# A stored table of priorities in place of a 60-pass search that orders the instructions of a two-layer encoder trunk

## The chip, the core and the metric

The kernel runs on one core of one Trainium2 chip. The metric is the device time of one execution, in microseconds. Lower is better.

## The reference

Two layers (DEPTH = 2) over 2048 frames of width 1024, all float32. Each layer normalises and modulates the frame, projects it once, mixes in two parallel groups of heads and adds the result to the residual:

```python
for l in range(DEPTH):
    mod = c_act @ w_ada[l] + b_ada[l]                       # shift, scale, gate
    h = rms_norm(x, norm_g[l]) * (1.0 + scale[:, None]) + shift[:, None]
    proj = h @ w_in[l]
    gq, gk, gv, glr, gz, dq, dk, dv, dz = split_columns(proj)
    gqkv = silu(causal_depthwise_conv(concat([gq, gk, gv]), conv_w[l]))
    o_gla  = gla_branch(...)    # 4 heads, chunks of 64: state = a*state + k_dec^T v ; o = q state ; rms_norm * silu(gz)
    o_diff = diff_branch(...)   # 4 heads, two softmax maps: p0 - lam*p1, block-causal ; rms_norm * silu(dz)
    x = x + gate[:, None] * (concat([o_gla, o_diff]) @ w_out[l])
```

## The kernel before

**Tiling.** The sequence is cut into NU = 4 units of 512 frames, so there are 8 unit passes (layer, unit). In each pass the normalised input stands as eight 128x512 tiles, each split into a high and a low part (`hhi`, `hlo`), and so is each weight tile (`w` holds both). A product in near-float32 precision is three matmuls: hi by hi, hi by lo, lo by hi. They add up in PSUM banks called `acc` (4 of them). Four more banks with the tag "tp" are shared by score tiles (`sc`), transposes (`tp`, matmuls against `ident`) and attention outputs (`po`).

**Streams.** Generators write the work down: the projections and the output projection (`acc<-...`); the gated linear attention (gate matmuls with `wglr`, cumulated gates with `trir`, transposes of `uT`, state products `sc<-vN,E` and `po<-Sn,qT`); the softmax attention of one head after another (scores `sc<-Kj,qh`, evicted by VectorE to `s` with a running minimum `mx`, exponential on ScalarE, transposes `tp<-ident,s`, their copy on ScalarE, then `po<-Vj,s` and `po<-Vt,s`; the result is scaled into `z` by a power `wq` that GpSimd makes, and transposed, `tp<-ident,z`, into `oh` and `ol`); the preparation of the next unit (`xt` is squared on ScalarE for the norm, `xp` times the norm gives `hhi`, `hlo`); and the modulation (`wr` loads multiplied into `am` on VectorE). In unit 0 of layer 0 the first norm is made in a special start: squares summed into `sqs`, a matmul with `ones`, `xms`, a power on GpSimd, `t` (a diagonal), a broadcast matmul, `rsb`, and the first modulation from `wm`.

**What sets the order.** Nothing of this is issued when it is written down. `Program.record` stores each operation with its dependencies, its buffers and a cost from a formula; there are 19,414 of them. `order(turn_of)` then runs a list scheduler over a model of the five queues: at each step the engine that is free first takes, among its operations that are ready, the one with the smallest number in `turn_of`. A tile is given a buffer when its turn in its pool has come, so pools bound how far work can run ahead. The order that comes out is issued as it is; each engine then works through its own list in that order, and waits where an operand is late. Loads and stores all stand in one list on SyncE's queue.

```python
            while pend[e] and pend[e][0][0] <= t:
                heapq.heappush(avail[e], heapq.heappop(pend[e])[1:])
```

In the kernel before, `turn_of` starts as the order of writing and is changed in 60 passes (`best_order`): where the model shows TensorE waiting, the chain behind the wait is moved up; a pass whose modelled span isn't longer is kept. All engine instructions of the computation carry the line of the one call in `issue` (L375 before, L351 in the changed kernel), so groups are told apart by tile names.

Of the kernel before, what the change touches and what calls it, by code (L numbers as in the profile page):

```python
# [4 lines left out]

# [11 lines left out]
AF = mybir.ActivationFunctionType  # L17
ALU = mybir.AluOpType
AX = mybir.AxisListType
# [3 lines left out]
P = 128  # L23
D = 1024
KT = D // P
UT = 512
TT = UT // P
# [23 lines left out]
class View:  # L51
# [57 lines left out]
    def real(self):  # L109
        ap = self.buf.tile  # L110
        for name, args, kw in self.path:
            ap = getattr(ap, name)(*args, **kw)
        return ap
# [10 lines left out]
class Program:  # L124
# [90 lines left out]
        func = op[2][2] if op[1] == "activation" else None  # L215
        return {AF.Exp: 0, AF.Tanh: 0, AF.Ln: 1}.get(func)

    def best_order(self, rounds=60):


        ops, rnd = self.ops, random.Random(0)
        turn = [float(i) for i in range(len(ops))]
        made = self.order(turn)
        best = self.span
        for _ in range(rounds):
            res, begin, end, ready, held = made
            lines = {e: [i for i in res if ops[i][0] == e] for e in "TAV"}
            place = {i: k for q in lines.values() for k, i in enumerate(q)}
            waits = [(begin[i] - end[j], i) for j, i in zip(lines["T"], lines["T"][1:]) if begin[i] - end[j] > 150]
            turn2 = list(turn)  # L230
            for wait, i in waits:
                if rnd.random() >= wait / 1500 * rnd.random():
                    continue
                first = begin[i] - 15000
                for _ in range(12):
                    e = ops[i][0]
                    i = max(ops[i][4] | {held.get(i, i)} - {i}, key=lambda j: end[j] + self.LAT[ops[j][0]][e], default=None)
                    if i is None or end[i] < first:
                        break
                    if (ops[i][0] in "AV" or ops[i][0] == "T" and i not in self.group) and begin[i] - ready[i] > 80:  # L240
                        q, k = lines[ops[i][0]], place[i] - 1
                        while k >= 0 and begin[q[k]] >= ready[i]:
                            turn2[i] = min(turn2[i], turn[q[k]] - 0.5)
                            k -= 1
            made2 = self.order(turn2)
            if self.span <= best:
                best, made, turn = self.span, made2, turn2
        self.span = best
        return made[0]

    def order(self, turn_of):
        ops, N = self.ops, len(self.ops)
# [114 lines left out]

    def issue(self):
        real = lambda v: v.real() if isinstance(v, View) else v
        for i in self.best_order():  # L370
            e, method, args, kw, _, _, bufs = self.ops[i]
            for b in bufs:
                if b.tile is None:
                    b.make()
            getattr(self.engines[e], method)(*[real(a) for a in args], **{k: real(v) for k, v in kw.items()})  # L375
# [988 lines left out]
        lam=np.stack([lam_q1, lam_k1, lam_q2, lam_k2], axis=1).reshape(1, -1))  # L1364


# [19 lines left out]
```

## Time and profile before

| what | value |
|---|---|
| median of 3 runs | 2448.12 us (2446.68 to 2451.21) |
| profiled execution | 2444.97 us, its span 2443.3 us |
| mean granted TensorE clock | 0.994 |
| TensorE busy | 2375.5 us (97%), 12903 matmuls |
| VectorE, ScalarE, GpSimd busy | 1828.8, 1240.2, 124.3 us |
| DMA | 573.77 MB, mean 235 GB/s |

An instruction's row gives engine, tile names (out<-in), shape and count. An fp32 product with a 128-column operand (`po`, the 64-row state products) appears as two matmuls each. The idle time of TensorE is what the span leaves beside its busy time; a matmul's row lasts longer than the distance to the next one's start, so short waits do not show as idle.

### The profile page before, as it was taken

How to read it: one execution, taken by the hardware profiler on the slowest of the kernel's cores; microseconds unless marked ns; L12 is line 12 of the kernel's file. 1: busy time of each engine (PE TensorE's matmuls, PEld its weight loads, DVE VectorE, ACT ScalarE, POOL GpSimd, SP SyncE). 2: the span in 40 equal slices, each digit the busy share in tenths (PEclk: the TensorE clock that was granted, in tenths of full speed). 3: DMA queues.
4: the chain of work that ended last, by engine and by line, in shares of the span. 5: the costliest groups of instructions: out<-in, count | busy, mean ns of one | idle time of the engine just before them, and what ended most of it. 6: DMA issues, size and time to landing. Idle time of an engine off the chain costs nothing.

```text
span 2443.3 us, 38591 instructions
## 1 busy us (share of the span) xinstructions
PE 2375.5 (97%) x12903; PEld 1941.1 (79%) x12903; DVE 1828.8 (75%) x5166; ACT 1240.2 (51%) x2726; POOL 124.3 (5%) x400
## 2 busy tenths in 40 slices
PE   6899899999999999999999999999999999999998
PEld 5687687887888878887788877888788887888787
DVE  8878776897568976589875887468864888738883
ACT  4776643566345553355664566255532555425442
POOL 0010000000000000000000010000000000000000
PEclk9899999999999999999999999999999999999999
DMA  7657897777766869487567877675686776866663
GB/s 298 234 208 253 283 341 249 238 260 250 250 228 207 253 192 300 162 243 210 189 219 272 287 249 261 228 242 191 221 273 215 233 226 220 248 227 203 195 206 126
DMA packets 369526, 573.77 MB, mean 235 GB/s; under 512 B 191824, under 2 KB 251696, under 8 KB 366256
## 3 DMA queue, kind: packets, MB, share of 16 engines
q1 hardware_dynamic: 369328, 571.32, 70.7%
q8 instruction: 102, 1.67, 0.3%
q14 instruction: 96, 0.79, 0.1%
HBM read 416.03 MB, written 161.50 MB: 236 GB/s over the span
## 4 chain that ended last, share of the span: by engine, by line
PE 75%; DVE 13%; DMA 5%; ACT 4%; issue 2%; POOL 0%; SPq 0%; POOLq 0%; DVEq 0%; ACTq 0%
PE acc L375 50%; PE sc L375 11%; PE po L375 9%; DVE s L375 6%; PE tp L375 4%; DMA wr<-in_w_ada_dram 2%; DVE t L375 1%; ACT s L375 1%; DVE w L375 1%; DMA xt<-in_x_dram 1%; ACT qh L375 1%; DVE am L375 0%; ACT t L375 0%; DVE r L375 0%; DMA xp<-xd 0%
## 5 line engine op out<-in xcount | busy, mean ns | idle before, releaser
L375 PE MATMUL acc<-w,hhi 128*128 128x512 f32 x2560 | 831.5, 401 | 5.9 <-ACT hhi L375 2.3
L375 PEld LDWEIGHTS acc<-w,hhi 128*128 128x128 f32 x2560 | 467.9, 189 | 98.2 <-DVE t L375 3.9
L375 PE MATMUL acc<-w,hlo 128*128 128x512 f32 x1280 | 507.3, 397 | 0.0
L375 ACT ACTIVATE s<-s,mx 128x512 f32<-128x512 f32 (+15 forms) x256 | 308.2, 1204 | 302.2 <-DVE s L375 152.7
L375 PE MATMUL acc<-oh,w 128*128 128x512 f32 x1024 | 357.7, 400 | 2.3 <-ACT oh L375 0.8
L375 DVE TENSOR_SCALAR_CACHE_REDUCE s<-sc,mx 64x64 f32<-64x64 f32 (+5 forms) x640 | 307.4, 483 | 48.1 <-PE sc L375 27.6
L375 PE MATMUL acc<-hhi,w 128*128 128x512 f32 x960 | 318.9, 398 | 0.0
L375 PEld LDWEIGHTS acc<-w,hlo 128*128 128x128 f32 x1280 | 241.9, 189 | 49.3 <-issue 1.1
L375 PEld LDWEIGHTS acc<-oh,w 128*128 128x128 f32 x1024 | 192.5, 189 | 44.4 <-DVE rt L375 3.2
L375 PEld LDWEIGHTS acc<-hhi,w 128*128 128x128 f32 x960 | 179.5, 188 | 36.3 <-DVE z L375 0.6
L375 PE MATMUL acc<-ol,w 128*128 128x512 f32 x512 | 201.9, 394 | 0.0
L375 PEld LDWEIGHTS po<-Vj,s 128*128 128x128 f32 x1536 | 193.4, 196 | 8.6 <-DMA s<-ad 1.7
L375 DVE SCALAR_TENSOR_TENSOR s<-s,r 128x512 f32<-128x512 f32 (+2 forms) x320 | 198.3, 666 | 2.3
L375 PE MATMUL po<-Vj,s 128*128 128x128 f32 x1536 | 198.5, 281 | 1.0 <-ACT s L375 0.7
L375 PE MATMUL acc<-hlo,w 128*128 128x512 f32 x480 | 189.0, 394 | 0.0
L375 DVE TENSOR_SCALAR_CACHE_REDUCE s<-sc 128x512 f32<-128x512 f32 (+4 forms) x256 | 157.9, 621 | 38.3 <-PE sc L375 29.0
L375 PE MATMUL sc<-Kj,qh 128*128 128x512 f32 x384 | 161.2, 420 | 6.0 <-DVE s L375 5.9
L375 PE MATMUL sc<-Kj,ql 128*128 128x512 f32 x384 | 152.2, 396 | 0.0
L375 ACT CAST w<-raw 128x512 fp32r<-128x512 f32 x160 | 97.8, 622 | 104.7 <-PE acc L375 84.1
L375 DVE TENSOR_TENSOR w<-raw,w 128x512 fp32r<-128x512 f32 x160 | 108.8, 686 | 45.9 <-ACT w L375 45.1
L375 DVE SCALAR_TENSOR_TENSOR t<-ub,vec,t 128x512 f32<-128x512 f32 x192 | 138.1, 746 | 6.0 <-ACT t L375 5.5
L375 POOL MEMSET s<- 64x64 f32 x256 | 36.9, 144 | 2020.0 <-PE po L375 1405.6
(185 smaller groups left out, 3590.2 us busy)
## 6 DMA issues: line engine op xcount, KB each, us to landing
w<-wd SPq DMA_DIRECT2D x416, 512.0 KB, 4.4
wd<-w SPq DMA_DIRECT2D x144, 512.0 KB, 4.1
raw<-in_w_all_dram SPq DMA_DIRECT2D x80, 512.0 KB, 4.8
Kj<-kd SPq DMA_DIRECT2D x48, 512.0 KB, 6.0
ad<-s SPq DMA_DIRECT2D x24, 768.0 KB, 5.6
s<-ad SPq DMA_DIRECT2D x24, 768.0 KB, 6.9
wr<-in_w_ada_dram SPq DMA_DIRECT2D x128, 128.0 KB, 4.3
ad<-s SPq DMA_DIRECT2D x32, 512.0 KB, 3.6
```

Source lines behind the costliest of these rows:

```text
L375: getattr(self.engines[e], method)(*[real(a) for a in args], **{k: real(v) for k, v in kw.items()})
```

## The change

`best_order` is gone. `found_order` unpacks a stored table of 19,414 small numbers, one for each recorded operation, sums them up and adds them to the order of writing; the result is `turn_of` for one call of `order`. The scheduler, its costs, the pools, the recorded operations, their number and their operands are unchanged; only the place of each in its engine's list differs.

```diff
-    def best_order(self, rounds=60):
-        ops, rnd = self.ops, random.Random(0)
-        turn = [float(i) for i in range(len(ops))]
-        made = self.order(turn)
-        best = self.span
-        for _ in range(rounds):
...
-            made2 = self.order(turn2)
-            if self.span <= best:
-                best, made, turn = self.span, made2, turn2
-        self.span = best
-        return made[0]
+    def found_order(self):
+        step = np.frombuffer(lzma.decompress(base64.b85decode(ORDER)), dtype="<i2")
+        turn = np.arange(len(self.ops), dtype=float)
+        if len(step) == len(turn):
+            turn += np.cumsum(step.astype(int))
+        return self.order(turn.tolist())[0]
...
-        for i in self.best_order():
+        for i in self.found_order():
...
+ORDER = (
+    '{Wp48S^xk9=GL@E0stWa8~^|S5YJf5;FqgLq+I|2U>bnck+!@@V3AjytBp45^Tr3;$E~Z9ORR0R@5I(P6(V1^7&ZjV2!e;h2L-hkd023f?~QmHvy'
...
```

On TensorE 5,222 of the 11,215 recorded operations keep their order among themselves; half of all stand at least 20 places away from where they stood. On VectorE it is 2,211 of 4,254 (half moved by 5 places or more), on ScalarE 1,210 of 2,313 (4), on SyncE 738 of 1,236 (3), on GpSimd 360 of 396. Both lists load ScalarE's tables 17 times. Three places, on which the prediction rests:

**The start, on VectorE**, from the last sums of squares (`sqs`) to the first `xp` and `hlo`. `wm` is the modulation, `w<-raw,w` the low part of a weight tile. Before:

```order
L375 TENSOR_TENSOR sqs<-t_195,sqs 128x512
L375 SCALAR_TENSOR_TENSOR wm,sv<-wm,cb 128x1024 x2
L375 TENSOR_SCALAR xms<-sc 128x4
L375 TENSOR_TENSOR B_217<-sv,vec 128x1
L375 SCALAR_TENSOR_TENSOR sv<-sv,vec 128x1
L375 TENSOR_TENSOR w<-raw,w 128x512
L375 TENSOR_TENSOR A_226<-sv,vec 128x1
L375 TENSOR_TENSOR w<-raw,w 128x512
L375 TENSOR_SCALAR t_231<-ident,rs_115 128x128 x4
L375 TENSOR_TENSOR w<-raw,w 128x512 x2
L375 SCALAR_TENSOR_TENSOR wm,sv<-wm,cb 128x1024
L375 SCALAR_TENSOR_TENSOR xp<-xp,A_226,rsb 128x512
```

Now:

```order
L351 TENSOR_TENSOR sqs<-t_205,sqs 128x512
L351 SCALAR_TENSOR_TENSOR wm,sv<-wm,cb 128x1024 x2
L351 TENSOR_TENSOR w<-raw,w 128x512 x2
L351 TENSOR_SCALAR xms<-sc 128x4
L351 SCALAR_TENSOR_TENSOR sv<-sv,vec 128x1
L351 TENSOR_TENSOR B_232<-sv,vec 128x1
L351 TENSOR_TENSOR A_235<-sv,vec 128x1
L351 TENSOR_SCALAR t_239<-ident,rs_105 128x128 x4
L351 SCALAR_TENSOR_TENSOR wm,sv<-wm,cb 128x1024 x2
L351 SCALAR_TENSOR_TENSOR xp<-xp,A_235,rsb 128x512
```

Two `w` steps have moved ahead of `xms` (two others, not shown, ahead of the sums of squares), and the second pair of `wm` steps stands ahead of the first `xp` as a whole, where one of them stood before.

**The end of the first unit, on TensorE**, at the gate matmuls of the second unit (`wglr`), which need its `hhi` and `hlo` one after another. Before:

```order
L375 MATMUL acc<-w,hlo 128x512
L375 MATMUL tp<-ident,vN 128x128
L375 MATMUL acc<-w,hhi 128x512
L375 MATMUL tp<-ident,vN 128x128 x7
L375 MATMUL sc<-hhi,wglr_550 32x512
L375 MATMUL sc<-hlo,wglr_550 32x512
```

Now:

```order
L351 MATMUL acc<-w,hhi 128x512
L351 MATMUL sc<-hhi,wglr_368 32x512
L351 MATMUL acc<-w,hlo 128x512
L351 MATMUL acc<-w,hhi 128x512 x2
L351 MATMUL acc<-w,hlo 128x512
L351 MATMUL sc<-hlo,wglr_368 32x512
L351 MATMUL sc<-hhi,wglr_368 32x512
L351 MATMUL sc<-hlo,wglr_368 32x512
L351 MATMUL acc<-oh,w 128x512
L351 MATMUL acc<-ol,w 128x512
```

Projection matmuls of the first unit and of its output now stand ahead of and between the gate matmuls; the last `hhi` is first read some 47 matmuls of 512 columns later than before, while its making on ScalarE is the 342nd activation in place of the 347th.

**The last head, on TensorE**: the last attention outputs, the transposes of `z`, and the output projection (`acc<-oh,w`). Before:

```order
L375 MATMUL po<-Vj,s 128x128 x4
L375 MATMUL tp<-ident,z 128x128
L375 MATMUL po<-Vt,s 128x128 x4
L375 MATMUL tp<-ident,z 128x128 x3
L375 MATMUL acc<-oh,w 128x512 x4
```

Now:

```order
L351 MATMUL po<-Vt,s 128x128 x4
L351 MATMUL tp<-ident,z 128x128 x3
L351 MATMUL acc<-ol,w 128x512
L351 MATMUL acc<-oh,w 128x512 x3
L351 MATMUL acc<-ol,w 128x512
L351 MATMUL acc<-oh,w 128x512 x2
L351 MATMUL tp<-ident,z 128x128
L351 MATMUL acc<-ol,w 128x512
```

Seven matmuls of the output projection now stand between the last `po` and the last transpose of `z`, and more of them follow it.

More of the change, by code (lines that the diff above doesn't have):

```diff
@@ L1 @@
+import base64
 import heapq
+import lzma
 import math
-import random
 from contextlib import ExitStack
@@ L216, in table @@
         return {AF.Exp: 0, AF.Tanh: 0, AF.Ln: 1}.get(func)
-    def best_order(self, rounds=60):
-        ops, rnd = self.ops, random.Random(0)
-        turn = [float(i) for i in range(len(ops))]
-        made = self.order(turn)
-        best = self.span
-        for _ in range(rounds):
[L226 to L244, printed above, removed]
-            made2 = self.order(turn2)
-            if self.span <= best:
-                best, made, turn = self.span, made2, turn2
-        self.span = best
-        return made[0]
+    def found_order(self):
[4 more added lines that the diff above has]
+        return self.order(turn.tolist())[0]
     def order(self, turn_of):
```

203 lines of the change are left out of this document (added).

## The prediction

> **What bounds the kernel now.** I read the page's first lines, then the stretches of dense matmuls, then the idle time of TensorE by stages, then who ended its waits.
>
> ```profile
> PE 2375.5 (97%) x12903; PEld 1941.1 (79%) x12903; DVE 1828.8 (75%) x5166; ACT 1240.2 (51%) x2726; POOL 124.3 (5%) x400
> PE   6899899999999999999999999999999999999998
> PEclk9899999999999999999999999999999999999999
> ```
>
> TensorE is the bound: 67.8 us of the span are left beside its busy time. The change alters no instruction, so only that time, time at a lowered clock and what hides inside "busy" can change. What hides is seen by the pace, in the chain that ended last (start, length, engine, tile, count) and the group of the commonest matmul:
>
> ```profile
> 1838.00 24.54 PE acc L375 x108
> 2178.80 0.44 PE tp L375 x4
> 2106.96 0.11 PE tp L375
> 2114.69 2.82 PE po L375 x24
> 2109.85 0.22 PE po L375 x2
> L375 PE MATMUL acc<-w,hhi 128*128 128x512 f32 x2560 | 831.5, 401 | 5.9 <-ACT hhi L375 2.3 <-ACT ub L375 1.7 <-DVE t L375 1.2
> ```
>
> A 512-column matmul starts 227 ns after the last (24.54/108), but its row lasts 401 ns. A wait thus shows as idle only beyond 174 ns. By stages (us; TensorE busy, matmuls, granted clock, DMA share, GB/s):
>
> ```profile
> 24.00:61.00 37.00, 37.00 (x158) 1.00 0.68 265
> 61.00:88.00 27.00, 26.95 (x124) 1.00 0.67 229
> 88.00:126.00 38.00, 27.05 (x109) 0.73 0.57 215
> 126.00:244.00 118.00, 116.59 (x688) 1.00 0.69 237
> 244.00:285.00 41.00, 34.51 (x149) 0.92 0.77 273
> 285.00:2397.00 2112.00, 2089.80 (x11461) 1.00 0.72 235
> 2397.00:2443.30 46.30, 39.17 (x206) 0.96 0.40 145
> ```
>
> Idle: 11.0 us in 88 to 126, 1.4 to 244, 6.5 to 285, 22.2 in the whole middle, 7.1 in the tail; the first 24 us hold the other 19.5. The lowered clock costs another 0.27 x 38 = 10.3 us, 0.08 x 41 = 3.3 us and 0.04 x 46.3 = 1.9 us. A first unit with little work beside it, and a middle of many small waits: that is all there is to win.
>
> **The change, term by term**, against the profiled execution (span 2443.3 us, 2444.97 us with what lies around it; the median of the runs is 3.15 us above that).
>
> *A, the start.* Rows of the timeline (start, length):
>
> ```profile
> 14.62 1.87 PE L375 MATMUL sc<-ones,sqs 128*128 128x1 f32 x8 [14.62 <-DVE sqs L375]
> 16.97 0.15 DVE L375 TENSOR_SCALAR xms<-sc 128x4 f32<-128x4 f32 x1
> 17.18 0.69 DVE L375 TENSOR_TENSOR w<-raw,w 128x512 fp32r<-128x512 f32 x1
> 20.77 1.22 DVE L375 SCALAR_TENSOR_TENSOR wm<-wm,cb 128x1024 f32<-128x1024 f32 x1
> 21.91 0.75 DVE L375 SCALAR_TENSOR_TENSOR xp<-xp,A,rsb 128x512 f32<-128x512 f32 x1
> 23.47 0.80 PE L375 MATMUL acc<-w,hhi 128*128 128x512 f32 x1 [2.27 <-ACT hhi L375]
> ```
>
> `xms` follows its matmul at once. Now two `w` steps stand before it: 2 x 0.69 = 1.4 us on the chain to the first projection. Behind the diagonal `t` two `wm` (2 x 1.22) stand where two `w` and one `wm` stood (2 x 0.69 + 1.22): about even. The two `w` moved ahead of the sums fall into VectorE's wait for `cb`, whose load now stands first on SyncE's queue. I take +1.5 us (first projection matmul near 25.0), from 0 (all hidden by the earlier loads) to +3.
>
> *B, 61 to 126.*
>
> ```profile
> 98.56 1.06 ACT L375 ACTIVATE xt<-xt 128x1024 f32<-128x1024 f32 x1 [2.23 <-DMA xt<-in_x_dram]
> 108.07 1.06 ACT L375 ACTIVATE xt<-xt 128x1024 f32<-128x1024 f32 x1 [2.41 <-DMA xt<-in_x_dram]
> 109.25 0.17 DVE L375 TENSOR_SCALAR xms<-xss 128x4 f32<-128x4 f32 x1 [1.28 <-ACT xt L375]
> 109.97 0.45 PE L375 MATMUL tp<-ident,s 128*128 128x128 f32 x1 [5.48 <-DVE s L375]
> ```
>
> ScalarE stands twice before loads of `xt`, and VectorE's `xms` behind them holds up the eviction that frees the scores' bank. In the new order that `xms` stands behind the eviction and behind the reciprocal-root steps of the second head, and an exponential that stood behind the first of these squares stands ahead of it. But the exponentials of `E` still follow the last square, and its load stands three places later on SyncE's queue. I take less than half of the 21.3 us of idle time and clock: -9, from -17 to +5 if the load comes later still.
>
> *C, 126 to 285.*
>
> ```profile
> 258.69 0.42 PE L375 MATMUL sc<-hhi,wglr 128*32 128x512 f32 x1 [1.72 <-DVE ol L375]
> 259.80 0.63 PE L375 MATMUL sc<-hhi,wglr 128*32 128x512 f32 x1
> 260.22 0.63 PE L375 MATMUL sc<-hlo,wglr 128*32 128x512 f32 x1
> 266.23 0.64 PE L375 MATMUL sc<-hhi,wglr 128*32 128x512 f32 x1 [2.09 <-ACT hhi L375]
> ```
>
> The gate matmuls come one by one as `hhi` is made, partly at half pace (0.42 us apart). Now some 47 matmuls, 47 x 0.227 = 10.7 us, lie between where TensorE stood and the last of these, and `hhi` isn't made later. The stage's 7.9 us of idle time and 3.3 us of clock go but for 3: -8 (-11 to 0).
>
> *D, the middle.* The waits that show are short and spread:
>
> ```profile
> PE sc L375 <- DVE s L375: 8.3, 9, 1.7
> PE acc L375 <- ACT ub L375: 1.7, 2, 1.3
> PE po L375 <- ACT s L375: 1.6, 3, 0.8
> ```
>
> Counted from the starts of the 11461 matmuls against the paces above, 236 starts are late by over 0.1 us, 54.8 us in all. For each I compared the TensorE work that lies between the waiting matmul and the last one its operands come from. In 22.0 us of them that cover grew by at least the wait, in 14.7 it didn't, and 18.0 wait for a bank, where I can't say; scores are now more often parted by projection matmuls, so I count a third, 6. -28, from -45 to +5.
>
> *E, the tail.*
>
> ```profile
> 2409.73 0.38 PE L375 MATMUL tp<-ident,z 128*128 128x128 f32 x2
> 2411.75 0.33 PE L375 MATMUL tp<-ident,z 128*128 128x128 f32 x1 [1.63 <-DVE z L375]
> 2412.86 1.77 PE L375 MATMUL acc<-oh,w 128*128 128x512 f32 x4 [0.78 <-ACT oh L375]
> ```
>
> The seven matmuls (1.6 us) put before the last `z`, and those behind it, cover both waits, and with them most of the 1.9 us of clock: -4 (-5 to 0).
>
> *F, more switching.* TensorE's list has more single transposes and single `po` among projections. A lone transpose took 0.11 us as in four (0.44); two lone `po` halves 0.22 against 0.235 in 24. 0, from -3 to +5.
>
> *G, new thin covers.* The state products now stand as little as 1.1 us of work behind the transposes of `vN` (2.8 before), with this copy between:
>
> ```profile
> L375 ACT COPY vN<-tp 128x512 f32<-128x512 f32 x32 | 18.6, 581 | 17.4 <-PE tp L375 17.1
> ```
>
> Enough if ScalarE is free, else 0.2 to 0.5 us at each of 16 bursts: +8 with other thin places (0 to +15).
>
> *H, weight loads*, the term most against the change.
>
> ```profile
> w<-wd SPq DMA_DIRECT2D x416, 512.0 KB, 4.4
> PE acc L375 <- DMA w<-wd: 0.3, 1, 0.3
> DMA to landing us min/median/max: 2.6/4.4/8.0
> ```
>
> Before, one load made TensorE wait, 0.3 us. Between the last use of the tile that frees a buffer and the first use of the tile loaded into it lay 9.5 us of TensorE work in the median, 6.1 in the leanest twentieth, under 5.0 at 3 of 416 loads. Now it is 7.8, 5.0, and 28 loads. Against landings of 4.4 (up to 8.0) I take 28 x 0.2 = +6 (0 to +30).
>
> The reload of turned attention weights gains cover (21.0 to 24.2 us in the median) and costs nothing; ScalarE's list loads its tables as often as before.
>
> Sum: 1.5 - 9 - 8 - 28 - 4 + 0 + 8 + 6 = -33.5. Span 2409.8, execution 2411.5, median 2414.6: **2415 us**.
>
> The clock is the place to weigh a rule. In the rows of C the half pace came after waits of 1.72 us and less, with a few matmuls between; B's and C's clock loss goes only if such clusters go, and I keep half of B's. The Trainium skill ("TensorE: Matmul & The Clock Gate", the part on the HAM clock gate) puts the halving after a whole idle window of about 3.4 us. By that rule no stall as short as C's would cost clock, and B's 10.3 us would all go once its 5.48 us wait falls below the window: some 5 us less than the sum, inside the likeliest case. The trace speaks against it in C: 0.92 granted with no wait over 2.1 us.
>
> **The rivals.**
> - *Nearly all waits go*: B, C and E in full, D's 54.8 but for 10, nothing at G and H: 1.5 - 17 - 11 - 45 - 5 = -76 at most, 2372; with half of that beyond the sum, about 2390. For it: the new order keeps projections as fillers at all three places shown. Against: 14.7 us in D have no better cover. 0.15.
> - *Given back*: D gains its bare 22, and G and H take their upper ends: 1.5 - 9 - 8 - 22 - 4 + 15 + 30 = +3.5, some 2451. For it: the leanest weight loads all lost cover. Against: before, even covers of 6.1 us cost nothing. 0.08.
> - *Slower, by the weight loads alone*: a quarter of the 416 loads now has under 6.1 us of cover. If 104 loads come late by 0.38 us, 39.5 us eat all that A to G give; it decides from there, and at 0.6 us (62 us) the time is some 2471. For it: landings reach 8.0 us. Against: the median of 4.4 and DMA at 0.72 of its time. 0.08.
> - *The table isn't used* (its length unlike the list's): then the order of writing would be issued. Its length is 19,414, as the operations; 0.
>
> **How the numbers follow.** Likeliest, 2400 to 2430: 0.54; the first rival, below 2400: 0.15; a smaller gain, 2430 to 2443, where B and D give half: 0.15; given back, 0.08; slower, 0.08. Within 0.2% (4.9 us) a measurement can't tell the two kernels apart. So faster 0.84, same 0.08, slower 0.08. The range 2388 to 2445 leaves out some 0.06 below and 0.12 above.
>
> **What would show it.** TensorE's 67.8 us of idle time falls to some 45. First projection matmul near 25.0 (A). The wait before the first transposes of `s` near 110 under 3 us, the clock of that stage above 0.8 (B). No wait over 1 us at `wglr` (C). Waits of scores for VectorE's `s` below half of 8.3 us (D). None over 0.5 us at the last `z` (E). Waits of `acc` for `w<-wd`: some us in place of 0.3 (H); if they pass 20 us, or if B's stage keeps its 11 us, the prediction is wrong.

## The result, and the profile after

The changed kernel takes 2431.9 us (median of 4 runs, 2430.82 to 2434.48) against 2448.52 (4 runs of the kernel before on the same chip): ratio 0.9933, interval 0.9916 to 0.995. It is faster by 16.6 us, half of the 33 forecast, and inside the range. The profiled execution takes 2430.82 us, its span 2428.7. The page's first lines, the stages, and who ended TensorE's waits (us in total, times, longest), all of the changed kernel:

```profile
PE 2372.0 (98%) x12903; PEld 1945.9 (80%) x12903; DVE 1829.6 (75%) x5166; ACT 1230.7 (51%) x2726; POOL 125.6 (5%) x400
PE   6899999999999999999999999999999999999999
PEclk9899999999999999999999999999999999999999
```

```profile
24.00:61.00 37.00, 34.78 (x143) 1.00 0.65 252
61.00:88.00 27.00, 27.00 (x125) 1.00 0.65 225
88.00:126.00 38.00, 25.72 (x113) 0.79 0.66 229
126.00:244.00 118.00, 115.85 (x679) 0.99 0.66 236
244.00:285.00 41.00, 39.95 (x204) 1.00 0.92 333
285.00:2397.00 2112.00, 2097.08 (x11512) 1.00 0.72 233
2397.00:2428.70 31.70, 27.76 (x123) 0.99 0.60 215
```

```profile
PE sc L351 <- DVE sqs L351: 17.0, 1, 17.0
PE tp L351 <- ACT E L351: 9.7, 2, 9.3
PE acc L351 <- DVE t L351: 2.9, 2, 1.8
PE sc L351 <- DVE s L351: 2.6, 6, 1.1
PE acc L351 <- DMA w<-wd: 2.3, 6, 0.7
```

TensorE idles 56.7 us in place of 67.8. The stage of 244 to 285 has its clock back (0.92 to 1.00) and 204 matmuls in place of 149; the stage of 88 to 126 has 12.3 us of idle time (11.0 before) and a clock of 0.79 (0.73); the start is later; scores wait 2.6 us for `s` in place of 8.7; weight loads cost 2.3 us. The gate matmuls and the last transpose of `z` stand without a wait:

```profile
274.36 0.39 PE L351 MATMUL sc<-hhi,wglr 128*32 128x512 f32 x1
279.21 0.39 PE L351 MATMUL sc<-hlo,wglr 128*32 128x512 f32 x1
2398.73 0.33 PE L351 MATMUL tp<-ident,z 128*128 128x128 f32 x1
```

Idle rows hide short waits, so the rest of this document goes by a **ledger**: how late each matmul starts against the sum of the paces of all matmuls ahead of it in its list (227 ns for 512 columns and so on, as in the prediction). What this lateness grows by between two amounts of TensorE work done (us of work) is what that stretch loses to waits, low clock and slow matmuls. It can be worked out in the same way for every run:

```
work done   0-80  80-200  200-240  240-1020  1020-1120  1120-1900  1900-2240  2240-end   sum
before      41.6    11.5     11.8      35.1       10.2       25.6       17.6       6.1  159.6
changed     44.7     9.5      1.1      29.4       13.7       32.3       13.8       0.5  145.1
e1          44.1     8.8      1.4      28.3       12.3       29.1       13.0       0.5  137.5
h_aba       45.9     9.6      1.5      31.4       15.3       26.4       12.9       0.5  143.4
h_bab       42.8    11.9     11.5      37.7       17.0       29.7       19.9       4.5  175.1
e6          43.9     9.4      1.2      31.0       11.2       30.8       13.6       0.5  141.6
best1       43.6     8.2      1.3      29.8       11.8       27.4       13.5       0.5  136.1
```

The columns count work, not time: 80 us of work are done at some 125 us, so the first column holds the start and stage B (61 to 126 us) together; 200 us are done at some 254 us. The changed kernel gains at the second unit's gate (200 to 240), in the first layer and in the tail, loses at the start, at the beginning of layer 1 (1020 to 1120) and in most of layer 1. One and the same list differs from execution to execution: in 240 to 1020 the three rows that share the new list there have 29.4, 31.4 and 31.0 us, and two runs that aren't in the table, e3 and best4, lose some 4 us more there than the changed kernel. A difference of a few us in one column shows little by itself.

### The profile page after: what moved, and what is told of

Its sections match the earlier page's. It is cut to its first block, busy times and chain, and to the rows that moved or that the text cites. A ratio compares the mean times of both kernels' runs of the same rounds, so it can differ in the third digit from the quotient of the medians.

```text
span 2428.7 us, 38475 instructions
## 1 busy us (share of the span) xinstructions
PE 2372.0 (98%) x12903; PEld 1945.9 (80%) x12903; DVE 1829.6 (75%) x5166; ACT 1230.7 (51%) x2726; POOL 125.6 (5%) x400
## 4 chain that ended last, share of the span: by engine, by line
PE 78%; DVE 11%; ACT 4%; DMA 4%; issue 2%; POOL 0%; SPq 0%; DVEq 0%; ACTq 0%; POOLq 0%
PE acc L351 52%; PE sc L351 12%; PE po L351 9%; PE tp L351 5%; DVE s L351 4%; DMA w<-wd 2%; ACT s L351 1%; DVE w L351 1%; DVE t L351 1%; DVE xp L351 1%; ACT la L351 1%; DMA xp<-xd 1%; DVE vN L351 1%; DVE hlo L351 1%; DMA wr<-in_w_ada_dram 1%
## 5 line engine op out<-in xcount | busy, mean ns | idle before, releaser
L351 PE MATMUL acc<-w,hhi 128*128 128x512 f32 x2560 | 844.8, 405 | 7.0 <-DVE t L351 2.9
L351 PE MATMUL acc<-w,hlo 128*128 128x512 f32 x1280 | 496.5, 402 | 0.3 <-DVE hlo L351 0.3
L351 ACT ACTIVATE s<-s,mx 128x1280 f32<-128x1280 f32 (+15 forms) x256 | 308.3, 1205 | 317.0 <-DVE s L351 201.5
L351 PE MATMUL acc<-oh,w 128*128 128x512 f32 x1024 | 335.9, 398 | 2.0 <-DMA w<-wd 1.6
L351 PEld LDWEIGHTS po<-Vj,s 128*128 128x128 f32 x1536 | 215.6, 196 | 13.7 <-issue 0.6
L351 PE MATMUL po<-Vj,s 128*128 128x128 f32 x1536 | 221.8, 280 | 0.0
L351 DVE SCALAR_TENSOR_TENSOR s<-s,r 128x512 f32<-128x512 f32 (+3 forms) x320 | 201.2, 666 | 3.6
L351 DVE TENSOR_TENSOR w<-raw,w 128x512 fp32r<-128x512 f32 x160 | 108.1, 685 | 33.5 <-ACT w L351 32.8
```

## The experiments

**The bursts.** What the forecast had at nothing, F, shows first. The 16 state products of a burst (two rows each) stand in the list of the kernel before as written, so that neighbours use other row halves of the array; the new table mixes them. TensorE's timeline before, and in the changed kernel:

```profile
207.51 1.10 PE L375 MATMUL sc<-vN,E 64*64 64x128 f32 x32
213.54 1.10 PE L375 MATMUL po<-Sn,qT 64*64 64x128 f32 x32
```

```profile
214.82 1.58 PE L351 MATMUL sc<-vN,E 64*64 64x128 f32 x32
222.40 1.38 PE L351 MATMUL sc<-vN,E 64*64 64x128 f32 x32
231.05 1.16 PE L351 MATMUL po<-Sn,qT 64*64 64x128 f32 x32
```

Before, 29 of the 32 bursts last 1.10 us; the other three hold waits inside, 2.5 us in all. In the changed kernel they last 1.10 to 1.59. From start to the next matmul's start the 32 bursts take 35.6 us before (19.1 for `sc`, 16.5 for `po`) and 41.4 now. e1 puts only the inner order back, in the changed kernel:

```diff
+        for i in made:
+            if i not in self.group:
+                out.append(i)
+            elif self.group[i] in bursts:
+                out += sorted(bursts.pop(self.group[i]))
```

> The changed kernel with one thing put back: the 16 small state matmuls of each of the 32 bursts are issued in the order in which they are written (neighbours in other row and column halves), at the place where the table puts the burst. Theory 1, the inner order costs: such a burst spans 1.03 us in the order written and 1.03 to 1.52 us in the table's, 41.3 against 35.6 us over the 32 bursts of sc and po, with the starts behind them some 7 us: the time falls by 6 to 8 us, to 2424 to 2426, and the bursts all take 1.03 to 1.07 us again. Theory 2, the gain was lost to late operands and weight loads: the bursts grow shorter and TensorE waits behind them instead, 2430 to 2433.

Measured: 2426.1 us, ratio 0.991 (0.9896 to 0.9923). The bursts:

```profile
214.15 1.10 PE L360 MATMUL sc<-vN,E 64*64 64x128 f32 x32
229.51 1.10 PE L360 MATMUL po<-Sn,qT 64*64 64x128 f32 x32
```

They take 33.2 us in all, 8.2 less; the ledger falls by 7.6 us, spread over nearly all stretches. By ratios the gain is 0.23% (5.6 us), and the intervals overlap a little, so the rows carry this more than the times. e2 does the opposite in the kernel before: each burst in the order of odd members, then even ones.

```diff
+            for k, i in zip(places, members[1::2] + members[0::2]):
+                made[k] = i
```

> The kernel before with one thing changed: inside each of the 32 bursts of 16 state matmuls, those written at odd places are issued first, then those at even places, so that neighbours lie in the same half. Theory 1, the inner order costs: each burst takes 1.52 in place of 1.03 us, 32 x 0.49 = 15.5 us, so 2464 (2460 to 2466) against 2448.5. Theory 2, the cost per matmul is the same in every order and the long bursts in the changed kernel are late operands: 2448.5, no change.

Measured: 2458.5 us, 1.0047 (1.0035 to 1.006), slower by 10.7 us. 30 of the 32 bursts take 1.52 us, two some 2.2 with a wait inside (50.1 in all, 14.5 more). The time lies under theory 1's 2460 to 2466; that a part of the bursts' cost falls into waits that stood behind them before is likely, but not shown. That the inner order costs holds in both directions. e8 asks which neighbour costs, with four inner orders in one kernel (places within each four of a burst).

```diff
+            kinds = (None, ((0, 3), (2, 1)), ((0, 2), (1, 3)), ((0,), (2,), (1,), (3,)))[n // 2 % 4]
```

> The kernel before, with the inner order of the 32 bursts cycling through four patterns, eight bursts each: (a) as written, row halves alternate and column halves change at every second step; (b) row halves alternate, the column half stays for eight matmuls; (c) the row half stays for eight, column halves alternate; (d) row and column half stay for four matmuls. Theory 1, only a neighbour in the other row half lets the weight load run beside the matmul: a and b 1.03 us a burst, c and d 1.52; in all 16 x 0.49 = 7.8 us more than before, about 2455. Theory 2, the neighbour must differ in both halves: a some 1.03, b, c and d 1.5. Theory 3, any other quarter of the array will do: only d is slow; e2's 1.52 us a burst speak against it.

One run: 2462.3 us. Bursts of the kinds a, b, c, d:

```profile
214.42 1.10 PE L389 MATMUL po<-Sn,qT 64*64 64x128 f32 x32
219.80 1.59 PE L389 MATMUL sc<-vN,E 64*64 64x128 f32 x32
487.12 1.59 PE L389 MATMUL sc<-vN,E 64*64 64x128 f32 x32
503.28 2.56 PE L389 MATMUL sc<-vN,E 64*64 64x128 f32 x32
```

From start to the next matmul's start a takes 1.034 us in the median, b and c 1.521, d 2.494. Theory 2 has a, b and c; no theory has d. A quarter of the array comes round again after four matmuls in a, after two in b and c, at once in d: the sooner, the slower. The Trainium skill ("TensorE: Matmul & The Clock Gate", the part on packing small matmuls) says that a weight load overlaps with matmuls in flight only when its row group differs. Pattern c, and e2, agree; pattern b, where every neighbour has the other row half, is as slow as c, so here that alone isn't enough.

**Is a gain local?** Two kernels join the lists: one with the new list, from 1154 us (in layer 0's last unit) the old one, from 2039 us the new one again; and its mirror.

```diff
+        lists = (made, other, made)
+        for op, rest in ((9562, lists[1]), (16474, lists[2])):
+            head = lists[0][:lists[0].index(op)]
+            done = set(head)
+            lists = (head + [i for i in rest if i not in done],) + lists[1:]
+        made = lists[0]
```

Here `other` is the list of the kernel before.

> The changed kernel, but from the last units of layer 0 (1154 us) to 2039 us the instructions come in the order of the kernel before, and behind that in the new order again. Theory 1, the table's gain is local to its first half and its tail and its middle is worse than the old one: from the ledger of starts against paces the changed kernel leads by 18.4 us at the first seam, loses 13.7 us between the seams, and gains 9.8 us after them; with the old list between them the lead is 28.2 us, so 2418 to 2422 with 0 to 3 us for the seams. Theory 2, the loss in the second half is what a lead in the first half turns into with any list (weights and buffers that come no faster): 2430 to 2434.

> The mirror image: the kernel before, with the changed kernel's order between the same two seams. Theory 1, the ledger holds piece by piece: 13.7 us slower than before, 2460 to 2465. Theory 2, the middle of the table loses only what the first half had gained: no change, 2446 to 2450.

h_bab: 2461.1 us, 1.0057 (1.0043 to 1.007), 13.3 us slower where 13.7 was worked out. h_aba: 2427.9 us, 0.9919 (0.9906 to 0.9933), by the ratios 3.4 us better than the changed kernel and not 14, with intervals that overlap. From 1120 to 1900 the old list loses 26.4 us there, as in the kernel before (25.6) and not as in the new list (32.3), so that part of the gain is local; about half of it would be the bursts again, since e1, the new list with sorted bursts, loses 29.1 there. Of the rest, 3.7 us were lost ahead of the seam, where the list is the changed kernel's own, and most went at the first seam, where neither list alone waits so long:

```profile
1158.71 0.33 PE L393 MATMUL tp<-ident,z 128*128 128x128 f32 x1 [1.14 <-DVE z L393]
1165.37 0.80 PE L393 MATMUL sc<-Kj,qh 128*128 128x512 f32 x1 [5.55 <-DVE s L393]
```

**The beginning of layer 1.** In the changed kernel the stretch from 1194 us holds no projection matmul for 20 us. Its windows, with those around it; then the kernel before where its own layer 1 begins, and h_bab, which comes there with the new list behind the old one; then the changed kernel's first rows:

```profile
1170.00:1194.00 24.00, 24.00 (x138) 1.00 0.72 238
1194.00:1214.00 20.00, 17.63 (x82) 0.74 0.15 54
1214.00:1230.00 16.00, 16.00 (x99) 1.00 0.68 248
```

```profile
1170.00:1214.00 44.00, 43.45 (x237) 1.00 0.62 198
1218.00:1240.00 22.00, 19.27 (x98) 0.92 0.21 73
```

```profile
1196.88 0.50 PE L351 MATMUL sc<-Kj,qh 128*128 128x512 f32 x1 [0.26 <-DVE s L351]
1197.98 0.47 PE L351 MATMUL sc<-Kj,qh 128*128 128x512 f32 x1 [0.37 <-DVE s L351]
1199.74 1.31 PE L351 MATMUL sc<-t,trir 128*128 128x512 f32 x2 [1.06 <-ACT t L351]
1200.85 0.63 PE L351 MATMUL sc<-Kj,qh 128*128 128x512 f32 x1
1201.28 0.63 PE L351 MATMUL sc<-Kj,ql 128*128 128x512 f32 x1
```

Pairs of scores come every 1.1 us, as VectorE evicts them, and after the wait for `t` they run at half pace (0.43 us apart): 2.4 us of idle time and 0.26 x 20 = 5.2 us of clock. How long the half pace lasts changes with the execution: 10.2 us here, 3.4 and 6.8 us in e1 and e3, whose lists are the same there but for the bursts. e6 takes the old list for this place alone (1154 to 1272 us), with the joined list given once more to `order` as priorities, so that it smooths the seams.

```diff
+        for op, rest in ((9562, lists[1]), (10348, lists[2])):
...
+        made = lists[0]
+        rank = [0.0] * len(made)
+        for k, i in enumerate(made):
+            rank[i] = float(k)
+        made = self.order(rank)[0]
```

> The changed kernel, but where layer 1 begins (from 1154 us to some 1272 us) the instructions follow the list of the kernel before, smoothed at both seams by the recorder's own model. Theory 1, the table is worse at this one place, a cluster of waits and half clock at 1192 to 1204 us: between the seams the changed kernel loses 12.6 us against the paces and the kernel before 4.5, so the time falls by 8 us less 0 to 3 for the seams, 2424 to 2427 against 2431.9. Theory 2, the lead of the first half is spent at the layer's start whatever the list: 2430 to 2433.

Measured: 2429.5 us, 0.9927 (0.9914 to 0.9941): 1.5 us, not 8. The cluster is gone; in its place TensorE waits just behind the seam. The windows of e6:

```profile
1154.00:1194.00 40.00, 36.55 (x194) 1.00 0.59 186
1194.00:1214.00 20.00, 20.00 (x116) 1.00 0.31 109
```

Every version loses 10 to 17 us between 1020 and 1120 us of work, the kernel before 10.2 (most of it before 1060). By the time that is nearer to theory 2, but "whatever the list" isn't shown. Behind 1060 the kernel before loses only some 3 us, and h_bab, with the new list and without the lead, has the cluster again and loses some 10: the cluster goes with the new list. What the old list loses instead behind the changed kernel's first half, by the lead or by the seam itself, stays open.

**The start of the second unit's attention, stage B.** Before the transposes of `s` TensorE now waits 9.3 us. The chain in the changed kernel, from VectorE's last reader of `la` over SyncE's loads and ScalarE to TensorE:

```profile
100.43 0.69 DVE L351 TENSOR_TENSOR t<-la,t 128x512 fp32r<-128x512 f32 x1
101.18 0.33 SPq L351 DMA_DIRECT2D xt<-in_x_dram  x1
106.89 0.33 SPq L351 DMA_DIRECT2D xt<-in_x_dram  x1
112.22 1.06 ACT L351 ACTIVATE xt<-xt 128x1024 f32<-128x1024 f32 x1 [4.07 <-DMA xt<-in_x_dram]
114.14 0.45 PE L351 MATMUL tp<-ident,s 128*128 128x128 f32 x1 [9.26 <-ACT E L351]
```

`la`, the `xt` tiles and `E` take turns in the four buffers of one pool. The table reads `la` for the last time at 100.43 in place of 93.25 us; the next `xt` load follows at once (101.18), the last one after its square (106.89, before 99.74), the exponentials of `E` after that, and `E` frees the bank that the transposes need. e5 makes only that reader, the matmul behind it and the load late, in the kernel before.

```diff
+        for i, j in ((580, 613), (582, 613), (540, 613)):
+            made.remove(i)
+            made.insert(made.index(j), i)
```

> The kernel before with one part of the change alone: the last reader of the gate tile la on VectorE (the second copy t<-la, 93.25 us), the matmul behind it and the load of the third x tile, whose buffer la holds, come later by some 2.8 us, as the changed kernel has them later by 6.7. Theory 1, the wait before the transposes of s near 110 us is the end of a chain of buffers (la, x tile, square, x tile, square, E, bank): it moves by what the load moves, from 5.5 to some 8.3 us, TensorE starts again near 112.8 us, and the time grows by 2 to 4.5 us. Theory 2, as predicted, the wait is set by the TensorE work laid over it: nothing changes, 5.5 us and 2446 to 2450.

Measured: 1.0009 (0.9999 to 1.0018), 2450.9 us; the loads go at 97.03 and 104.45 us (before: 94.42 and 99.74), and the growth of the time, some 2 us by the ratio, isn't clear of the noise. ScalarE and TensorE:

```profile
110.60 1.08 ACT L379 ACTIVATE E<-sc 128x512 f32<-128x512 f32 x2
111.34 0.45 PE L379 MATMUL tp<-ident,s 128*128 128x128 f32 x1 [5.50 <-ACT E L379]
```

`E` starts 1.35 us later than before (109.25) and TensorE goes on 1.37 us later (109.97): the end of the wait follows `E`. It doesn't follow `xms` on VectorE or the eviction of `s` behind it, as the prediction had read it: in e5 these start at 111.74 and 112.01 us, when TensorE already runs again (in the kernel before, at 109.25 and 109.53, they ended so close to `E` that the row there names `s`). But it moved by half of what theory 1 said (ScalarE's own work lay beside the load), and the wait kept its 5.5 us because the moved matmul had made TensorE wait 1.2 us earlier. So the chain is shown by the rows, its price by this run only in part. An order with `la` freed early in the changed kernel, or a buffer of its own for `xt`, wasn't tried.

**The start, stage A.** Rows of the changed kernel: ScalarE's first square, then TensorE:

```profile
10.32 0.63 ACT L351 ACTIVATE t<-xp 128x512 f32<-128x512 f32 x1 [2.34 <-DMA xp<-in_xl_dram]
17.02 1.87 PE L351 MATMUL sc<-ones,sqs 128*128 128x1 f32 x8 [17.02 <-DVE sqs L351]
22.02 2.08 PE L351 MATMUL tp<-t,ones 128*128 128x128 f32 x8 [3.13 <-DVE t L351]
26.31 0.80 PE L351 MATMUL acc<-w,hhi 128*128 128x512 f32 x1 [2.22 <-ACT hhi L351]
```

e3 moves the two `w` steps ahead of `xms` (109, 70) back behind `A0` (65), VectorE's first step of the modulation (where the expectation below says ScalarE's).

```diff
+        for i in (109, 70):
+            made.remove(i)
+            made.insert(made.index(65) + 1, i)
```

> The changed kernel with two steps of VectorE put back: the two preparations of w that the table puts ahead of the first squares' sum go behind ScalarE's first step again. Theory 1, VectorE's list sets the start: TensorE's first matmul comes 1.3 to 1.5 us earlier (17.0 to about 15.6 us, 14.6 in the kernel before), and the lead is still there when the stage at 61 us begins. Theory 2, the start waits for the first loads: the first matmul stays at 17.0 us.

One run, 2429.7 us. TensorE:

```profile
16.30 1.87 PE L355 MATMUL sc<-ones,sqs 128*128 128x1 f32 x8 [16.30 <-DVE sqs L355]
20.36 2.08 PE L355 MATMUL tp<-t,ones 128*128 128x128 f32 x8 [2.19 <-DVE t L355]
```

The wait for `t` falls from 3.13 to 2.19: the two steps cost 0.94 us. The first matmul comes 0.7 us earlier only because `xp` landed earlier in this execution. The five profiles with the old start have their first square at 7.9 to 8.1 us, the nine with the new one (best4's, partly undone, among them) at 9.6 to 11.2: theory 2, a late load. The ledger's 3 us at 80 are gone by 480 (68.0 us late against 66.9), in one execution, where the spread of one list can do as much.

**The sum.** best1 is h_aba with smoothed seams and sorted bursts; best2 has e3's start too; best3 has its first seam at 1175 us; best4 is best2 with the load of `raw` behind the four of `xp` and its preparations behind the squares.

```diff
+        for i, j in ((28, 27), (122, 108), (83, 108), (123, 55), (84, 55)):
+            made.remove(i)
+            made.insert(made.index(j) + 1, i)
```

> The changed kernel with the old list from 1154 to 2039 us, the seams smoothed by the recorder's model, and all bursts of state matmuls in the order written. Theory 1, gains add up: 28.2 us from the ledger of the three pieces, 3 to 4 us from the bursts outside the middle piece, 0 to 3 us back for the seams: 2416 to 2421. Theory 2, the seams cost what the unsmoothed pieces cost (8 us at the first): 2424 to 2428.

> As best1, with the start of e3 as well (VectorE's two preparations of w behind ScalarE's first step). Theory 1, the 3.0 us that e3 had gained by 61 us stay to the end: 2419 to 2420 beside 2422. Theory 2, a later wait takes them back, as e3's profile seemed to show at 400 to 520 us: 2422.

> As best2, with the first seam at 1175 us in place of 1154. Theory 1, of the 5.7 us that e6 and best1 lose just behind the first seam (1155 to 1180 us) most is a cost of the seam, since neither list loses it alone: with the seam in a stretch where neither list waits, 3 to 5 us less than best2, 2414 to 2417. Theory 2, the loss belongs to the beginning of layer 1, whatever the list: as best2, 2418 to 2421.

> As best2, with the rest of the start put back too: the load of raw that the table sets ahead of the four loads of xp goes behind them, and ScalarE's and VectorE's preparations of w from it go behind the squares. Theory 1, the late first matmul is the late landing of xp (ScalarE's first square at 10.2 to 10.3 us in the changed kernel and best2, 7.9 before): first matmul near 14.7 us in place of 16.9, first projection near 23.0 in place of 25.2, and the time falls by some 2 us to 2419 to 2420. Theory 2, the first projections then wait for their w: first matmul 14.7, the first projections break up, 2422 again.

best1: 2422.2 us, 0.9893 (0.988 to 0.9907), just above theory 1's range. best2: 2421.8, 0.9896 (0.9881 to 0.9911): e3's start isn't seen in the time. best3: 2422.7, 0.9894 (0.9877 to 0.991): the loss moved with the seam, from 1060 to 1090 us of work to 1090 to 1120. The time is theory 2's; a loss that goes along with the seam can as well be the seam's own, which stays open. best4: 2420.1, 0.9884 (0.9868 to 0.9901). The four can't be told apart; each beats both kernels, by the ratios 9 to 12 us under the changed one. best4's start, TensorE and ScalarE:

```profile
9.60 0.63 ACT L412 ACTIVATE t<-xp 128x512 f32<-128x512 f32 x1 [3.48 <-DMA xp<-in_xl_dram]
16.31 1.86 PE L412 MATMUL sc<-ones,sqs 128*128 128x1 f32 x8 [16.31 <-DVE sqs L412]
25.86 0.79 PE L412 MATMUL acc<-w,hhi 128*128 128x512 f32 x1 [3.42 <-ACT hhi L412]
```

The first matmul stayed at 16.3, not 14.7: the load of `raw` isn't the cause, or only a small part. The loads of `xp` now start as before (2.18 us); what still differs is that `cb` goes first and that the tile squared first is the second of the four. Which of them it is stays open. The last row is theory 2's: `hhi` waits.

## Why the prediction was right or wrong

- **A** (+1.5; measured +2.8 at the first projection, 26.31 against 23.47). The two `w` steps cost 0.94 us where 1.4 were reckoned. Mis-sized was the sentence that saw only gain in the loads' new order: the first square starts 2.4 us later (10.32 against 7.92), because `xp` lands later.
- **B** (-9; measured -2.4 from 61 to 126). The step that failed is "I take less than half". It rested on VectorE's `xms` holding up the eviction that frees the bank; `xms` did move behind the eviction, and the wait grew all the same, since its end follows `E`. The text had seen that the exponentials of `E` still follow the last square and that its load stands later, and had it only in the range's end. The wait grew from 5.5 to 9.3 us; only the clock gained (0.73 to 0.79). The chain through the pool had to be followed one link further, to when `la` is free.
- **C** (-8; measured -10.7 in the ledger's third column) and **E** (-4; measured -5.6 in the last) were right in mechanism and near in size: with some 10 us of projections over the gate matmuls the waits there and the lowered clock are gone, and so are the waits at the last `z`. No run takes these projections away alone.
- **D with G** (-28 + 8) failed, in a way that the sum hides. Of the 236 late starts (54.8 us), the same matmuls are late by 7.8 us now: 47 us went, far more than the 28 taken. But 208 other matmuls start late by over 0.1 us, 43.2 us in all, where G allowed 8. Some of these are old waits that now stand before another matmul; the largest group at one place, some 7.6 us, is the 20 us without projections at 1194. A list of the waits before shows which ones can go. It doesn't show which come: for that the new list had to be read for stretches without projections, not only at the places that waited before.
- **F** (0, from -3 to +5): some 6 to 8 us by rows (e1: 5.6 by ratio). Single transposes and single `po` were looked at; the inner order of the bursts wasn't. The model charges each of these matmuls the same in any order, so a search that goes by it has no reason to keep one (how the table was found isn't on record; `best_order` left the members of a burst as written).
- **H** (+6; 2.3 us idle): weight loads come late 6 times, by 0.7 us at most. The cover needed was nearer to the landing time than feared.

In sum, D, F, G and H were -14 in the forecast, and the stretches from 240 us of work to 2240 measure +0.7 (88.5 to 89.2). Bursts are 6.5 of that difference (e1: 82.7), the rest is new waits. A and B were -7.5 and measure +1.1 (the first two columns, 53.1 to 54.2), and the miss is mostly B's; C and E gave 4.3 more than forecast. That is the half of the gain that didn't come: 33.5 us were forecast, 14.5 are in the ledger's sum. That the time still lies inside the wide range is partly luck: D was 19 us too small and G 35 us too small, with opposite signs.

On the clock, the prediction weighed a rule: the Trainium skill ("TensorE: Matmul & The Clock Gate", the part on the HAM clock gate) puts the halving after a whole idle window of about 3.4 us. The kernel before agrees in stage B: its clock falls at 109.2 us, 4.7 us into the wait. The changed kernel doesn't: there the granted clock falls at 106.7 us, 1.8 us into the wait that begins at 104.9 (1.00 from 104.8 to 106.6 us, 0.50 from 108.0). Nor does 1194 to 1214, with a clock of 0.74 and no wait over 1.1 us.

## What to carry to other kernels

When a search over a model reorders a list, look first at what the model charges the same for every order: here the inner order of small matmuls, which the table scrambled at a cost of some 6 us. Price a new order by its own thin places (stretches without the work that covers, buffers that come free later), not by the waits of the old order alone: most of those went, and nearly as much came at other places. And a chain through buffers of one pool is followed back until an instruction is found that waits for no buffer.

## What the runs showed of the hardware

- Sixteen 64x64 state products take 1.034 us when the quarters of the array take turns, 1.521 when two alternate, in whichever direction they differ, and 2.494 when one is used four times running (e8).
- TensorE fell to half pace in a cluster of score matmuls with waits of 0.3 to 1.1 us between them (changed kernel: clock 1.00 from 1194 to 1197 us, 0.50 from 1200 to 1209). A low rate of work for some us was enough: six matmuls started between 1195.4 and 1199.7 us, an estimated 1.3 us of work at their paces.
